# Moving the places of the matmul operands in on-chip memory: other strides for activations and weight buffers

## The chip, the cores and the metric

The kernel runs on one core of one Trainium2 chip. The metric is the device time of one execution in microseconds (us). Of the kernel before, three runs took 974.05, 974.58 and 975.09 us; the median is 974.58 us.

## The reference

One decoder layer on 256 rows of 2048 numbers, in float32. One wide projection of the input feeds three attention branches, each of which is gated, projected back, weighted by a sigmoid gate and summed; one output projection and a layer norm end it.

```python
proj = x @ w_in                                   # 256 x 2048 times 2048 x 15632
aq, ak, av, alr, agate, bq, bk, bv, bgate, cq, ck, cv, cgate, mgate = split(proj)
ya = gated_linear_attention(aq, ak, av, log_sigmoid(alr @ gla_w_up + gla_b) / 16) * silu(agate)
yb = sliding_window_attention(bq, bk, bv, swa_sinks) * silu(bgate)
yc = block_attention(cq, ck, cv) * silu(cgate)
up = einsum('bsnw,nwd->bsnd', stack([ya, yb, yc]), w_branch)      # three times 256 x 1024 x 2048
merged = sum(sigmoid(mgate + b_merge) * up)
out = merged @ w_o                                # 256 x 2048 times 2048 x 2048
x = layer_norm(2 ** 0.25 * x + out, ln_g, ln_b)
```

Nearly all of the arithmetic is in the matrix products with w_in, w_branch and w_o, whose weights (some 174 MB) are read once.

## The kernel before

**Split operands.** To come near float32 with TensorE's shorter float32r products, each operand is held as a high part and a low part (the rest), and three of the four cross products are summed: high by high, high by low, low by high.

**Chunks.** The weights are cut into chunks of 512 KB (four k-slices of 128 rows by 256 columns, or two by 512; 260 columns for the linear attention's values), in the order of their use (`seq`). `emit_chunk` loads a chunk into a `wraw` buffer over SyncE's DMA queue (line 129), casts it on ScalarE into a `whi` buffer (line 130), and subtracts on VectorE into a `wlo` buffer (line 131). There are four `wraw` buffers and three each of `whi` and `wlo`, used in turn; loads and splits run two chunks ahead of the products.

**Products with the weights standing.** In `mm3` (lines 230 to 239) 128 columns of a weight slice are loaded into TensorE as the stationary operand, and the activations of that k-slice stream past them: for the high part of the weights 512 columns (the activations' 256 high columns, then their 256 low ones, line 236), for the low part the 256 high columns (line 238). I call one such high matmul and the low one behind it a pair. A chunk of four slices and 256 columns makes 8 pairs; there are 2080 pairs in the program, 384 of them with the branch outputs `ya`, `yb`, `yc` as activations (tile `pu`), 1696 with the input `xhl`.

**Products with the activations standing.** In `nmm` (lines 274 to 282) it is the other way round: 128 columns of activations stand (`xhl`, or `mhl`, the merged result), and the weights stream past: high, low, high (lines 278, 279, 280), 260, 512 or 256 columns each. These are the values `av` (384 matmuls of 260 columns), `cv` and the first three groups of the output projection `wo` (480 of 512), and its last two groups (192 of 256).

**Places in memory.** A tile's address is its offset in bytes in each partition of the on-chip memory. What the change touches is where an operand begins; the table gives this offset modulo 512, as the two built programs have it. A buffer's k-slices of 256 columns are 1024 bytes apart and those of 512 columns 2048, so they all begin at the buffer's own place; with 260 columns they are 1040 bytes apart, and each of the four begins 16 bytes further on.

| operand | before | after |
|---|---|---|
| `xhl` and `mhl`, 16 k-slices | 416, each (2048 apart) | 224 + 96 k modulo 512: 16 places (2144 apart) |
| `ya`, `yb`, `yc`, 8 k-slices | 416, each | 224, each |
| `whi` buffers in order of use | 224, 352, 288 | 448, 128, 32 |
| `wlo` buffers in order of use | 32, 160, 96 | 160, 352, 256 |
| `wraw` buffers in order of use | 288, 480, 416, 352 | 288, 64, 480, 384 |

**Side work.** The attention branches run as jobs in small steps between the chunks (`tick`); their loads and swaps of halves go over GpSimd's DMA queue, whose descriptors stand in a scratch region of the on-chip memory (16384 bytes of each partition).

Of the kernel before, what the change touches and what calls it, by code (L numbers as in the profile page):

```python
# [9 lines left out]
F32 = mybir.dt.float32  # L10
F32R = mybir.dt.float32r
# [6 lines left out]
P = 128  # L18
S = 256
D = 2048  # L20
KT = D // P
# [6 lines left out]
RANK = 16  # L28
NV = 260
KC = 4  # L30
NWARM = 8


@with_exitstack
def kernel(ctx: ExitStack, tc: tile.TileContext, xT: bass.AP, x: bass.AP, w_in: bass.AP,
                             w_up: bass.AP, gla_b: bass.AP, norm_g: bass.AP, sinks: bass.AP, b_merge: bass.AP,
                             w_branch: bass.AP, w_o: bass.AP, ln_g: bass.AP, ln_b: bass.AP, out: bass.AP):
    nc = tc.nc

    const = ctx.enter_context(tc.tile_pool(name="const", bufs=1))  # L40
    wraw = ctx.enter_context(tc.tile_pool(name="wraw", bufs=4))
    wlo = ctx.enter_context(tc.tile_pool(name="wlo", bufs=3))
    whi = ctx.enter_context(tc.tile_pool(name="whi", bufs=3))
    acts = ctx.enter_context(tc.tile_pool(name="acts", bufs=1))
    work = ctx.enter_context(tc.tile_pool(name="work", bufs=2))
    pp = ctx.enter_context(tc.tile_pool(name="pp", bufs=2, space=PSUM))
    pa = ctx.enter_context(tc.tile_pool(name="pa", bufs=4, space=PSUM))

    # The weight chunks in the order of their use; loads and splits run ahead of the products.
    seq = []  # L50

    def deep(cols):
        return 2 if cols == 512 else KC

# [45 lines left out]
    def load_x(k0, k1):  # L100
        xs = xst[:, k0:k1, :]
        nc.sync.dma_start(xs, xT[:, k0:k1, :])
        nc.scalar.copy(xhl[:, k0:k1, 0:S], xs)
        nc.vector.tensor_tensor(xhl[:, k0:k1, S:2 * S], xs, xhl[:, k0:k1, 0:S].bitcast(F32), op=ALU.subtract)

    def emit_chunk():
        i = state["in"]
        state["in"] += 1
        src, row0, col0, cols, name = seq[i]
        kc = deep(cols)  # L110

        def shaped(t):
            return t.rearrange("p (k c) -> p k c", c=cols)
        raw = shaped(wraw.tile([P, KC * NV], F32, tag="wraw", name=f"w{name}")[:, :kc * cols])
        if name.startswith("wo4_"):
            if not last:
                last["h"] = acts.tile([P, KT, 256], F32R, tag="y", name="wlasth", bufs=2)
                last["l"] = acts.tile([P, KT, 256], F32R, tag="y", name="wlastl", bufs=2)
            k0 = KC * int(name[4:])
            hi, lo = last["h"][:, k0:k0 + KC, :], last["l"][:, k0:k0 + KC, :]  # L120
        else:
            hi = shaped(whi.tile([P, KC * NV], F32R, tag="whi", name=f"h{name}")[:, :kc * cols])
            lo = shaped(wlo.tile([P, KC * NV], F32R, tag="wlo", name=f"l{name}")[:, :kc * cols])
        view = src[row0:row0 + kc * P, col0:col0 + cols].rearrange("(k p) c -> p k c", p=P)
        cuts = [0, 1, 2] if i < 2 else [0, kc]
        for a, b in zip(cuts, cuts[1:]):
            if name.startswith("aq_"):
                load_x(row0 // P + a, row0 // P + b)
            nc.sync.dma_start(raw[:, a:b, :], view[:, a:b, :])
            nc.scalar.copy(hi[:, a:b, :], raw[:, a:b, :])  # L130
            nc.vector.tensor_tensor(lo[:, a:b, :], raw[:, a:b, :], hi[:, a:b, :].bitcast(F32), op=ALU.subtract)  # L131
        ready.append((name, hi, lo))

    def next_chunk(name):
        while state["in"] < len(seq) and state["in"] <= state["out"] + AHEAD:
            emit_chunk()
        got, hi, lo = ready[state["out"]]
        assert got == name, (got, name)
        state["out"] += 1
        return hi, lo  # L140

    # Side work, cut in steps; one step of each running job is issued between two chunks.
    jobs = []

    def tick():
# [4 lines left out]
    def wait(n):  # L150
        for _ in range(n):
            yield 1
# [2 lines left out]
        while jobs:  # L155
            tick()

    xhl = acts.tile([P, KT, 2 * S], F32R, tag="x", name="xhl")
    xst = acts.tile([P, KT, S], F32, tag="y", name="xst", bufs=2)

    # The tensor engine's clock rises only while it is busy: keep it so until the first operands are there.
    wz = const.tile([P, 512], mybir.dt.bfloat16, name="wz")
    nc.vector.memset(wz, 0.0)
    pw = pa.tile([P, 512], F32, tag="pa", name="pw")
    for _ in range(NWARM):
        nc.tensor.matmul(pw, wz[:, 0:P], wz, start=True, stop=True)
# [6 lines left out]
    nc.gpsimd.tensor_copy(ones, onesf)  # L173
    onerow = const.tile([P, 1], F32, name="onerow")
    nc.gpsimd.memset(onerow, 1.0)
    # The low-rank gate's weights three times over the rows (high, low, high parts), zeros between.
    wup3 = work.tile([96, 512], F32, tag="r", name="wup3")
    nc.gpsimd.memset(wup3, 0.0)
    for i in range(3):
# [23 lines left out]
    for i in (0, 2):  # L203
        nc.gpsimd.affine_select(mska[:, i, :], mska[:, i, :], pattern=[[-1, P]], compare_op=ALU.is_ge,
                                fill=NEG, base=0, channel_multiplier=1)
    # [row, column]: 1 where column > row; where column >= row; where column < row
    trif = work.tile([P, P], F32, tag="q1", name="trif", bufs=4)
    tril = const.tile([P, P], F32, name="tril")
    triu = const.tile([P, P], F32, name="triu")
# [98 lines left out]
    for k in range(0, KT, 2):  # L308
        hi, lo = next_chunk(f"aq_{k // 2}")
# [16 lines left out]
    def gla_job():  # L326
# [15 lines left out]
            return hl  # L342

        def sums(hl, name):
            # Sums over the partitions, the same in each row.
            pd = pa.tile([P, 512], F32, tag="pa", name=f"pd{name}")
            for e in range(2):
                nc.tensor.matmul(pd, ones, hl[:, e, :], start=e == 0, stop=e == 1)
            return pd

        def diagonal(g):
            prod = work.tile([P, 512], F32, tag="z", name=f"qk{g}")
            hs = slice(2 * g, 2 * g + 2)
            nc.vector.tensor_tensor(prod.rearrange("p (h t) -> p h t", h=2), aq[:, hs, :], ak[:, hs, :], op=ALU.mult)
            hl = halves(prod, f"d{g}")
            yield from wait(2)
            pd = sums(hl, f"d{g}")
            nc.vector.tensor_tensor(atd[:, hs, :, :], pd.rearrange("p (h t i) -> p h t i", h=2, t=2),
                                    ident[:, None, None, :].to_broadcast([P, 2, 2, P]), op=ALU.mult)
            yield 1  # L360
# [40 lines left out]
        hl = halves(e1, "1")  # L401
        yield from wait(3)
        place(0, sums(hl, "1"))

        def prep(L):
# [87 lines left out]
    def front_job():  # L493
        yield from gla_job()
        while not done:
            yield 1
        yield from keys_job()
        yield from in_turn(swa_job, 8, 6)
# [16 lines left out]
    def keys_job():  # L515
        nc.gpsimd.dma_start(ksw[0:64, :], bkv[64:128, 0, :])
        nc.gpsimd.dma_start(ksw[64:128, :], bkv[0:64, 0, :])
        yield from wait(2)
        # A key tile's values as [low parts | high parts]
        pv = pa.tile([P, 2, 2, 64], F32, tag="pa", name="pvb")  # L520
        for t in range(2):
            nc.tensor.transpose(pv[:, t, :, :], bkv[:, 1, t * P:(t + 1) * P], ident)
        nc.scalar.copy(vz[:, :, :, 64:P], pv)
        nc.vector.tensor_tensor(vz[:, :, :, 0:64], pv, vz[:, :, :, 64:P].bitcast(F32), op=ALU.subtract)
        yield from wait(2)
        for g in range(2):
            for r in range(2):
                rows = slice(64 * r, 64 * r + 64)
                src = bkv[rows, 0, :] if g == r else ksw[rows, :]
                nc.scalar.copy(ks[rows, g, 0, :], src)  # L530
                nc.vector.tensor_tensor(ks[rows, g, 1, :], src, ks[rows, g, 0, :].bitcast(F32), op=ALU.subtract)
# [1 line left out]
    yb = acts.tile([P, 8, 2 * S], F32R, tag="y", name="yb", bufs=2)  # L533

    def swa_job(hp):
        # A head's queries stand over its 64 rows as their high and low parts: products with the keys' high
        # parts twice and low parts twice give all four terms.
        g = hp // 4
        c0 = 1024 + 512 * (hp % 2)
        qs = swaw[:, c0:c0 + 512].rearrange("p (j c) -> p j c", j=2)  # L540
# [1 line left out]
        for j in range(2):  # L542
            rows = slice(64 * j, 64 * j + 64)
# [53 lines left out]
        for j in range(2):  # L597
            rows, other = slice(64 * j, 64 * j + 64), slice(64 - 64 * j, P - 64 * j)
# [127 lines left out]
    drain()  # L726
    merge(2, yc)

    mhl = acts.tile([P, KT, 2 * S], F32R, tag="x", name="mhl")
    for dg in range(8):  # L730
        ks = slice(2 * dg, 2 * dg + 2)
        nc.scalar.activation(mhl[:, ks, 0:S], merged[dg], AF.Copy, scale=0.5)
# [48 lines left out]
    parts = [next_chunk(f"wo4_{h}") for h in range(KT // KC)]  # L781
# [41 lines left out]
```

## Time and profile before

| | |
|---|---|
| median of three runs | 974.58 us |
| the profiled execution, first to last instruction | 973.3 us |
| TensorE busy with matmuls | 956.5 us (98%) |
| TensorE's weight loads | 841.5 us (86%) |
| VectorE, ScalarE, GpSimd busy | 632.6, 500.6, 93.6 us |
| mean granted TensorE clock | 0.996 |

The profile is of one execution. Its span is the time between the first and the last instruction on the chip; the measured time of a run has a little more around it (the median is 1.3 us longer than this span). Matmuls overlap in the pipeline, so the duration of one (0.39 us for 512 columns) is longer than the step from its start to the next one's start; a pace is read from starts in the timeline.

### The profile page before, as it was taken

The page shows a single profiled execution, that of the slowest core. Times are in us where ns is not written, and L with a number is a line of the kernel's source. Part 1 is how long each engine was busy: PE and PEld are TensorE (multiplying, and loading weights), DVE is VectorE, ACT ScalarE, POOL GpSimd, SP SyncE. Part 2 cuts the span into 40 slices and gives each one's busy share as a digit, 9 for nine tenths or more (in the row PEclk, how much of TensorE's full clock was granted, in tenths as well). Part 3 has the DMA queues.
Part 4 walks back from the last instruction along what each step waited for, and adds up shares of the span by engine and source line. Part 5 has one row for each costly group of instructions (what it writes and reads, how often), then busy time and mean ns, then how long its engine had stood idle before and what let it go on. Part 6 is the DMA issues. An engine that isn't in the chain of part 4 may idle for free.

```text
span 973.3 us, 14360 instructions
## 1 busy us (share of the span) xinstructions
PE 956.5 (98%) x5598; PEld 841.5 (86%) x5598; DVE 632.6 (65%) x780; ACT 500.6 (51%) x735; POOL 93.6 (10%) x127
## 2 busy tenths in 40 slices
PE   8999999999999999999999999999999999999995
PEld 5899889998888888888888888888888888888885
DVE  6544698758878888855544456665656565585556
ACT  6443574457566666644444445654445454563341
POOL 8100000003112322310000000110000000000003
PEclk9999999999999999999999999999999999999998
DMA  9766666555766666567666666487666666655652
GB/s 301 203 180 192 175 174 173 149 138 152 206 179 183 180 171 185 174 217 195 187 186 190 194 190 179 130 259 217 195 190 185 190 193 194 189 179 187 195 181 87
DMA packets 164052, 180.64 MB, mean 186 GB/s; under 512 B 6048, under 2 KB 150336, under 8 KB 163472
## 3 DMA queue, kind: packets, MB, share of 16 engines
q1 hardware_dynamic: 161552, 174.02, 61.7%
q0 software_dynamic: 2144, 5.51, 1.8%
q8 instruction: 44, 0.72, 0.3%
q10 hardware_dynamic: 288, 0.20, 0.1%
q14 instruction: 24, 0.20, 0.1%
HBM read 176.43 MB, written 2.10 MB: 183 GB/s over the span
## 4 chain that ended last, share of the span: by engine, by line
PE 95%; DVE 3%; DMA 1%; SPq 0%; POOL 0%; issue 0%; ACT 0%; DVEq 0%
PE psmg L236 18%; PE psmg L238 9%; PE pu L236 9%; PE pu L238 4%; PE psbq L236 3%; PE psag L236 3%; PE pscg L236 3%; PE pscq L236 3%; PE psck L236 3%; PE pswo L278 3%; PE pswo L280 3%; PE pswo L279 3%; PE psbg L236 2%; PE psav L278 2%; PE psav L279 2%; PE psav L280 2%
## 5 line engine op out<-in xcount | busy, mean ns | idle before, releaser
L236 PE MATMUL psmg<-xhl,hmg 128*128 128x512 f32 x768 | 269.1, 394 | 0.0
L238 PE MATMUL psmg<-xhl,lmg 128*128 128x256 f32 x768 | 214.5, 279 | 0.0
L131 DVE TENSOR_TENSOR lmg<-wmg,hmg 128x1024 fp32r<-128x1024 f32 x96 | 120.1, 1251 | 79.3 <-ACT hmg L130 79.2
L236 PEld LDWEIGHTS psmg<-xhl,hmg 128*128 128x128 f32 x768 | 144.4, 188 | 30.9
L130 ACT CAST hmg<-wmg 128x1024 fp32r<-128x1024 f32 x96 | 100.6, 1048 | 105.4 <-PE psmg L236 33.4
L238 PEld LDWEIGHTS psmg<-xhl,lmg 128*128 128x128 f32 x768 | 144.5, 188 | 0.1
L131 DVE TENSOR_TENSOR lwb<-wwb,hwb 128x1024 fp32r<-128x1024 f32 x48 | 58.8, 1224 | 40.9 <-ACT hwb L130 40.8
L130 ACT CAST hwb<-wwb 128x1024 fp32r<-128x1024 f32 x48 | 50.2, 1047 | 52.8 <-PE psmg L236 34.8
L131 DVE TENSOR_TENSOR lwo<-wwo,hwo 128x1024 fp32r<-128x1024 f32 x28 | 34.2, 1222 | 27.5 <-ACT hwo L130 27.4
L130 ACT CAST hwo<-wwo 128x1024 fp32r<-128x1024 f32 x28 | 29.4, 1050 | 41.9 <-PE pswo L280 38.5
L278 PE MATMUL pswo<-hwo,mhl 128*128 128x512 f32 (+1 forms) x128 | 47.0, 367 | 0.0
L280 PE MATMUL pswo<-hwo,mhl 128*128 128x512 f32 (+1 forms) x128 | 46.8, 366 | 0.0
L279 PE MATMUL pswo<-lwo,mhl 128*128 128x512 f32 (+1 forms) x128 | 46.8, 365 | 0.0
L236 PE MATMUL psbq<-xhl,hbq 128*128 128x512 f32 x128 | 45.6, 398 | 0.0
L236 PE MATMUL psbg<-xhl,hbg 128*128 128x512 f32 x128 | 45.2, 394 | 0.0
L236 PE MATMUL pu<-ya,hwb 128*128 128x512 f32 x128 | 45.0, 393 | 0.0
L236 PE MATMUL pu<-yb,hwb 128*128 128x512 f32 x128 | 45.0, 394 | 0.0
L236 PE MATMUL psag<-xhl,hag 128*128 128x512 f32 x128 | 44.9, 393 | 0.0
L236 PE MATMUL pu<-yc,hwb 128*128 128x512 f32 x128 | 44.6, 392 | 0.0
L236 PE MATMUL pscg<-xhl,hcg 128*128 128x512 f32 x128 | 44.4, 392 | 0.0
L236 PE MATMUL pscq<-xhl,hcq 128*128 128x512 f32 x128 | 44.4, 392 | 0.0
L236 PE MATMUL psck<-xhl,hck 128*128 128x512 f32 x128 | 44.3, 391 | 0.0
(309 smaller groups left out, 2349.5 us busy)
## 6 DMA issues: line engine op xcount, KB each, us to landing
wmg<-in_w_in_dram SPq DMA_DIRECT2D x96, 512.0 KB, 3.8
wwb<-in_w_branch_dram SPq DMA_DIRECT2D x48, 512.0 KB, 3.5
wwo<-in_w_o_dram SPq DMA_DIRECT2D x32, 512.0 KB, 4.5
wav<-in_w_in_dram SPq DMA_DIRECT2D x16, 520.0 KB, 3.7
wag<-in_w_in_dram SPq DMA_DIRECT2D x16, 512.0 KB, 3.7
wbq<-in_w_in_dram SPq DMA_DIRECT2D x16, 512.0 KB, 3.8
wbg<-in_w_in_dram SPq DMA_DIRECT2D x16, 512.0 KB, 3.7
wcq<-in_w_in_dram SPq DMA_DIRECT2D x16, 512.0 KB, 3.8
```

The lines of the kernel that those rows point to most:

```text
L130: nc.scalar.copy(hi[:, a:b, :], raw[:, a:b, :])
L131: nc.vector.tensor_tensor(lo[:, a:b, :], raw[:, a:b, :], hi[:, a:b, :].bitcast(F32), op=ALU.subtract)
L236: nc.tensor.matmul(ps, hi[:, k, c], rhs[:, k0 + k, :], start=first and k == 0, stop=False, skip_group_check=True)
L238: nc.tensor.matmul(ps[:, 0:S], lo[:, k, c], rhs[:, k0 + k, 0:S], start=False, stop=last and k == kc - 1, skip_group_check=True)
L278: nc.tensor.matmul(ps[:, t, :cols], sh, hi[:, k, :], start=kk == 0, stop=False, skip_group_check=True)
L279: nc.tensor.matmul(ps[:, t, :cols], sh, lo[:, k, :], start=False, stop=False, skip_group_check=True)
L280: nc.tensor.matmul(ps[:, t, :cols], sl, hi[:, k, :], start=False, stop=kk == KT - 1, skip_group_check=True)
```

## The change

The activations' tiles `xhl` and `mhl` get rows of 536 numbers for each k-slice, of which 512 are used; the three kinds of weight buffers get 8 numbers more (4192 bytes in place of 4160). The scratch region of GpSimd's DMA queue is halved, and with it every tile behind it begins 8192 bytes earlier, before the other shifts. The lines that are left out below are comments that the change drops.

```diff
@@ -28,6 +28,8 @@
 RANK = 16
 NV = 260
 KC = 4
+WCOLS = KC * NV + 8
+XP = 2 * S + 24
 NWARM = 8
...
-        raw = shaped(wraw.tile([P, KC * NV], F32, tag="wraw", name=f"w{name}")[:, :kc * cols])
+        raw = shaped(wraw.tile([P, WCOLS], F32, tag="wraw", name=f"w{name}")[:, :kc * cols])
...
-            hi = shaped(whi.tile([P, KC * NV], F32R, tag="whi", name=f"h{name}")[:, :kc * cols])
-            lo = shaped(wlo.tile([P, KC * NV], F32R, tag="wlo", name=f"l{name}")[:, :kc * cols])
+            hi = shaped(whi.tile([P, WCOLS], F32R, tag="whi", name=f"h{name}")[:, :kc * cols])
+            lo = shaped(wlo.tile([P, WCOLS], F32R, tag="wlo", name=f"l{name}")[:, :kc * cols])
...
-    xhl = acts.tile([P, KT, 2 * S], F32R, tag="x", name="xhl")
+    xhl = acts.tile([P, KT, XP], F32R, tag="x", name="xhl")[:, :, 0:2 * S]
...
-    mhl = acts.tile([P, KT, 2 * S], F32R, tag="x", name="mhl")
+    mhl = acts.tile([P, KT, XP], F32R, tag="x", name="mhl")[:, :, 0:2 * S]
...
-    nc = bacc.Bacc("TRN2", target_bir_lowering=False, num_devices=1)
+    nc = bacc.Bacc("TRN2", target_bir_lowering=False, num_devices=1, dynamic_dma_scratch_size=8192)
```

The instructions of every engine, their order and what they wait for are the same before and after; only addresses differ.

## Rows read from the trace of the kernel before

**Rows 1.** The page: span, busy time and share of each engine.

```profile
span 973.3 us, 14360 instructions
PE 956.5 (98%) x5598; PEld 841.5 (86%) x5598; DVE 632.6 (65%) x780; ACT 500.6 (51%) x735; POOL 93.6 (10%) x127
```

**Rows 2.** The page: the chain that ended last, by engine.

```profile
PE 95%; DVE 3%; DMA 1%; SPq 0%; POOL 0%; issue 0%; ACT 0%; DVEq 0%
```

**Rows 3.** TensorE's waits: what for, us in total, times, longest.

```profile
PE psaq L236 <- ACT haq L130: 1.6, 2, 0.9
PE pw L166 <- DVE wz L163: 1.3, 1, 1.3
PE psbg L238 <- DVE lbg L131: 1.2, 1, 1.2
```

**Rows 4.** Matmul groups by shape: count, busy us, mean ns, idle before.

```profile
L236 PE MATMUL psmg<-xhl,hmg 128*128 128x512 f32 x768 | 269.1, 394 | 0.0
L238 PE MATMUL psmg<-xhl,lmg 128*128 128x256 f32 x768 | 214.5, 279 | 0.0
```

**Rows 5.** Timeline, TensorE: first pair of four chunks that follow each other.

```profile
267.37 0.39 PE L236 MATMUL psmg<-xhl,hmg 128*128 128x512 f32 x1
...
270.18 0.39 PE L236 MATMUL psmg<-xhl,hmg 128*128 128x512 f32 x1
...
272.91 0.39 PE L236 MATMUL psmg<-xhl,hmg 128*128 128x512 f32 x1
...
275.68 0.40 PE L236 MATMUL psmg<-xhl,hmg 128*128 128x512 f32 x1
```

**Rows 6.** Windows of these chunks: us, engines' busy us, granted clock, DMA share, GB/s.

```profile
267.37:270.18 2.81, 2.81 (x18) 2.46 (x17) 2.74 (x6) 2.69 (x9) 1.02 (x2) 1.00 0.78 215
270.18:272.91 2.73, 2.73 (x19) 2.42 (x17) 2.43 (x6) 1.95 (x6) 0.00 (x0) 1.00 0.81 206
272.91:275.68 2.77, 2.77 (x19) 2.44 (x17) 1.86 (x2) 1.05 (x1) 0.00 (x0) 1.00 0.34 71
```

**Rows 7.** Timeline, TensorE: first matmuls of two chunks of `av`, 24 apart.

```profile
77.28 0.28 PE L278 MATMUL psav<-hav,xhl 128*128 128x260 f32 x1
...
80.17 0.29 PE L278 MATMUL psav<-hav,xhl 128*128 128x260 f32 x1
```

**Rows 8.** Timeline, TensorE: 12 matmuls of `wo` with 512 columns.

```profile
893.94 0.40 PE L278 MATMUL pswo<-hwo,mhl 128*128 128x512 f32 x1
...
896.73 0.39 PE L278 MATMUL pswo<-hwo,mhl 128*128 128x512 f32 x1
```

**Rows 9.** Timeline, TensorE: `wo` with 256 columns: 24 matmuls, later 15.

```profile
947.03 0.28 PE L278 MATMUL pswo<-hwo,mhl 128*128 128x256 f32 x1
...
949.87 0.28 PE L278 MATMUL pswo<-wlasth,mhl 128*128 128x256 f32 x1
...
958.49 0.28 PE L278 MATMUL pswo<-wlasth,mhl 128*128 128x256 f32 x1
...
960.29 0.28 PE L278 MATMUL pswo<-wlasth,mhl 128*128 128x256 f32 x1
```

**Rows 10.** Groups of the splits: busy us, mean ns, idle before and its releaser.

```profile
L131 DVE TENSOR_TENSOR lmg<-wmg,hmg 128x1024 fp32r<-128x1024 f32 x96 | 120.1, 1251 | 79.3 <-ACT hmg L130 79.2
L130 ACT CAST hmg<-wmg 128x1024 fp32r<-128x1024 f32 x96 | 100.6, 1048 | 105.4 <-PE psmg L236 33.4
```

**Rows 11.** DMA issues: count, KB each, median us to landing; GpSimd's queue, the loads of x.

```profile
wmg<-in_w_in_dram SPq DMA_DIRECT2D x96, 512.0 KB, 3.8
swaw<-ql POOLq DMA_DIRECT2D x16, 64.0 KB, 2.0
q0 software_dynamic: 2144, 5.51, 1.8%
L742 POOL DMA_DIRECT2D hx<-in_x_dram x2: 582/597/612, 420.9 to 640.3; - x2
```

## The prediction

> **What bounds the kernel now.** I read the page's busy shares first, then the chain of waits, then TensorE's own waits, and then the pace of the matmuls in the timeline. TensorE is busy for 956.5 of 973.3 us [rows 1] and makes 95% of the chain that ended last [rows 2]. Its three longest waits for another engine sum to 4.1 us, 2.9 of them at the start [rows 3]. So the time is, but for the few per cent that the chain gives to others, the sum of the steps from one matmul's start to the next. The groups by shape show the two that dominate, 768 of 512 columns and 768 of 256 in the gates' products alone, with no idle time before them [rows 4], but their durations overlap and cannot be added; only starts can.
>
> The starts show what this change can touch. Four chunks of the gates' products follow each other, each of 8 pairs, and differ in nothing but the weight buffers they use [rows 5]. The first begins at 267.37 us and the second at 270.18: 2.81 us for 8 pairs, 351 ns each (buffers at 224 and 32). The second takes 2.73 us, 341 ns (352 and 160). The third takes 2.77 us, 346 ns (288 and 96). The same work at the same granted clock, 1.00 in all three windows [rows 6], has three paces 3% apart. Contention with the other engines does not order them: the fastest chunk ran beside the busiest DMA (share 0.81), the middle one beside the idlest (0.34) and the least work of VectorE and ScalarE (1.86 and 1.05 us) [rows 6]. What goes with the pace is the place of the weights against that of the activations, which begin at 416 in every k-slice. I take from this that the stream of activations and the load of the next weights disturb each other, by an amount that hangs on their places and on how far one is ahead of the other. Within a chunk all 8 pairs have the same places, and the pace settles.
>
> The Trainium skill says otherwise: in "SBUF — State Buffer", section "Who interferes with whom", TensorE has two independent read ports, one for the stream and one for the weight load, and never waits on another reader; and "TensorE: Matmul & The Clock Gate", section "Wait — 56ns, not 53.3ns?", gives N ÷ 2.4 GHz plus about 2.5 ns from start to start. By that a pair would be 215.8 + 109.2 = 325 ns at any place, and the change would be worth nothing. The trace does not agree: 341 to 351 ns, by buffer. What the rule leaves alive is the first rival below.
>
> **The change part by part.** No instruction moves, so the sum has one large term, TensorE's pace, and some that I put at nothing.
>
> *Pairs with xhl: 1696.* Now three settled paces, mean (2.81 + 2.73 + 2.77) / 24 = 346.3 ns [rows 5]. After the change the activations of slice k begin at 224 + 96 k, so no two pairs of neighbouring slices have the same relation, and no pace settles over a chunk. The trace has no pair of this kind, so I bound it. Below: all pairs as the fastest buffer now, 341 ns, which is 1696 × −5.3 = −9.0 us. Above: all as the slowest, 351 ns, 1696 × 4.7 = +8.0 us. The nearest rows between these are the matmuls with the activations standing. Those of `av` stream from weights whose slices begin 16 bytes apart, so they see four places in each chunk: 2.89 us for 24, 120.4 ns for 260 columns [rows 7]. Beside them, `wo` with 512 columns takes 2.79 / 12 = 232.5 ns [rows 8] and with 256 columns 2.84 / 24 = 118.3 ns [rows 9], one place to a chunk. A column thus costs (232.5 − 118.3) / 256 = 0.446 ns, and `av` cut to 256 columns would be 120.4 − 4 × 0.446 = 118.6 ns. So many places are neither better nor worse than one of the three, 118.6 against 118.3. They are a little better than the last group of `wo`, where both operands begin at 416 and the step settles at 1.80 / 15 = 120.0 ns [rows 9].
>
> Put together, a 512-column and a 256-column step of this kind make 232.5 + 118.6 = 351.1 ns, 4.8 ns above the pairs' mean now. This says that the settled pairs are somewhat luckier than the usual step, and that unsettled ones would drift towards the usual. But `wo` loads its weights from one tile all the time, and its 512-column steps have no low part between them, so I believe it by half: 348.7 ns, +2.4 ns, 1696 × 2.4 = +4.1 us.
>
> *Pairs with the branch outputs: 384.* `ya`, `yb` and `yc` keep one place, 224, and the buffers move against it, so these settle again, at other relations. Between 341 and 351 ns that is −2.0 to +1.8 us; I take 0, the mean of three unknown paces.
>
> *The 1056 matmuls with activations standing.* They change places too. The steps of [rows 7 to 9], cut to 256 columns, lie within 118.3 to 120.0 ns, so 576 short ones could move by some ±1 ns and 480 long ones by ±2: ±1.5 us, taken as 0.
>
> *Splits and loads.* The casts and subtractions write to other places, and the loads land at others. A subtraction takes 1.25 us and a cast 1.05 [rows 10] of a chunk's 2.77 us; a load lands in 3.8 us [rows 11] and is issued two chunks ahead. The cover is TensorE's chunk. If it went, say by a cast and a subtraction of twice the length, VectorE with its other work would become late; TensorE waited for a split once after the start, for 1.2 us [rows 3]. I put it at 0, with 0 to +2 us.
>
> *The halved scratch of GpSimd's queue.* It moves 2144 packets and 1.8% of the engines' time; its loads of x are issued at 420.9 and 640.3 us, hundreds of us before the residual needs them; the swaps of query halves land in 2.0 us [rows 11] and stand four steps ahead of their use, some 11 us. Even if each of the 16 swaps took twice as long, nothing would wait: 0.
>
> *Sum.* +4.1 us on the profiled execution's 973.3 us span, 977.4 us. The median of the runs is 1.3 us above that span, so I predict 974.6 + 4.1 = 978.7 us.
>
> **The rivals.**
>
> *No change: the mean over places is what it was.* The three settled paces would be a fair sample, each pair would just draw from the same range, and the slow ones pay for the fast. For it: `av`'s many places cost what `wo`'s three do, 118.6 against 118.3 ns. Against it: 232.5 + 118.6 is above the pairs' mean. By the skill's two pages above there would be no change either, for another reason. Time: 974.6, ±2 us. Chance 0.25.
>
> *Faster: the settled pace is a resonance, and many places break it.* The mechanism is that in a settled chunk the load of the next weights meets the stream in each pair at the same point, again and again; where the relation changes with k, a bad meeting is not repeated. For it: two of three buffers are slower than the third by 5 and 10 ns a pair, and the pace falls by steps of 5 ns as the buffers' places rise by 64 bytes, so that places further on may be better still; the last group of `wo` gets its 120.0 ns with everything at one place. Against it: `av` shows no such gain against 118.3 ns. It decides once more than half of the relations behave as the fastest does; if two thirds do, 1696 × 2/3 × −5.3 = −6.0 us, 968.6 us; if all do, with the branch outputs' pairs, −11.0 us, 963.6 us. Chance 0.33.
>
> *Slower in full.* The pairs with xhl go all the way to 351.1 ns, as the steps of `wo` and `av` have it: 1696 × 4.8 = +8.1 us, 982.7 us. It is the far end of my forecast. If a bad branch-output pace and the splits came on top, 1.8 + 1 us, it would be 985.5 us.
>
> **How the numbers follow.** Slower than before, by the forecast's mechanism in half or in full: 0.42. No change: 0.25. Faster: 0.33. The forecast's own range is 976.6 to 983. As both signs hold much of the chance, the range for 8 times in 10 goes over all cases: from 965.0, which leaves out the last tenth, near every pair at the fastest pace, to 984.5. A measurement of this kernel can tell 0.2% from no change, 1.95 us, so "within" is 972.6 to 976.5 us. The rival without change lies wholly in it, the two others almost wholly outside, so the chances are those of the cases.
>
> **What would show it.** In the profile after, TensorE should still be 98% busy and its waits the same few us; the pairs with xhl should no longer have three paces by buffer but steps that change from k-slice to k-slice, with a mean near 349 ns over a few chunks; those with the branch outputs should again settle, at three paces. A mean near 346 says no change, one below 345 the resonance. I am wrong in the mechanism if pairs with xhl still run evenly within a chunk, since then the places were not what made the three paces; or if TensorE's waits on the splits have grown, since then the cost lies on VectorE and ScalarE.

## The result, and the profile after

The changed kernel takes 982.12 us (four runs, 982.04 to 982.63) against 974.84 us for the kernel before: a ratio of 1.0076, 95% interval 1.0061 to 1.0090. It is slower by 7.3 us. I predicted 978.7 us, slower, with a range of 965.0 to 984.5.

The head of the page after answers to [rows 1]; the columns are the same.

```profile
span 980.4 us, 14360 instructions
PE 964.8 (98%) x5598; PEld 844.3 (86%) x5598; DVE 632.8 (65%) x780; ACT 500.4 (51%) x735; POOL 92.9 (9%) x127
```

TensorE's busy time has grown by 8.3 us, the other engines' by nothing that matters (VectorE 632.6 to 632.8 us, ScalarE 500.6 to 500.4). Its longest waits for other engines are the same three as in [rows 3], 3.5 us in all where they were 4.1:

```profile
PE psaq L238 <- ACT haq L132: 1.3, 1, 1.3
PE pw L168 <- DVE wz L165: 1.3, 1, 1.3
PE psbg L240 <- DVE lbg L133: 0.9, 1, 0.9
```

The two large groups answer to [rows 4] (after the change the lines of `mm3` are two further down); the last number before the idle time is the mean duration in ns:

```profile
L238 PE MATMUL psmg<-xhl,hmg 128*128 128x512 f32 x768 | 272.5, 397 | 0.0
L240 PE MATMUL psmg<-xhl,lmg 128*128 128x256 f32 x768 | 215.7, 281 | 0.0
```

The durations went from 394 to 397 and from 279 to 281 ns. The starts tell the pace. These are the first pairs of the four chunks of [rows 5] (268.39, 271.19, 273.99, 276.79), and between them three neighbouring pairs of the second chunk:

```profile
268.39 0.39 PE L238 MATMUL psmg<-xhl,hmg 128*128 128x512 f32 x1
...
271.19 0.39 PE L238 MATMUL psmg<-xhl,hmg 128*128 128x512 f32 x1
...
272.24 0.40 PE L238 MATMUL psmg<-xhl,hmg 128*128 128x512 f32 x1
...
272.60 0.39 PE L238 MATMUL psmg<-xhl,hmg 128*128 128x512 f32 x1
...
272.94 0.40 PE L238 MATMUL psmg<-xhl,hmg 128*128 128x512 f32 x1
...
273.99 0.40 PE L238 MATMUL psmg<-xhl,hmg 128*128 128x512 f32 x1
...
276.79 0.40 PE L238 MATMUL psmg<-xhl,hmg 128*128 128x512 f32 x1
```

Where [rows 5] had 2.81, 2.73 and 2.77 us for 8 pairs, all three steps are now 2.80 us, 350 ns a pair; and within the second chunk, pairs that follow each other take 0.36 and 0.34 us. The three paces are gone, the fast one with them. The steps are not random, though. The chunk at 268.39 takes 343, 350, 348, 354, 357, 353, 346 and 346 ns for its 8 pairs, and the chunk at 286.41, six chunks on, has the same buffers, and its activations' places are 8 × 96 = 768 bytes further on, a multiple of 256: it takes the same eight times to the nanosecond. Over all pairs in the trace that nothing interrupts, those with `xhl` have a mean of 346.5 ns before (1656 pairs) and 351.1 after (1655); those with the branch outputs 347.0 and 348.8. Added over the whole trace, the pairs with `xhl` have grown by 6.6 us (5.7 in the steps behind a high matmul, 0.9 in those behind a low one) and those with the branch outputs by 0.7 us; the matmuls with the activations standing have lost 0.3 us. The sum with the rest is 7.05 us, which is the two spans' 7.1 us.

### The profile page after: what moved, and what is told of

It reads as the page before. It is cut to its first block, busy times and chain, and to the rows that moved or that the text cites. A ratio compares the mean times of both kernels' runs of the same rounds, so it can differ in the third digit from the quotient of the medians.

```text
span 980.4 us, 14360 instructions
## 1 busy us (share of the span) xinstructions
PE 964.8 (98%) x5598; PEld 844.3 (86%) x5598; DVE 632.8 (65%) x780; ACT 500.4 (51%) x735; POOL 92.9 (9%) x127
## 4 chain that ended last, share of the span: by engine, by line
PE 94%; DVE 4%; issue 1%; ACT 0%; DMA 0%; POOL 0%; SPq 0%; DVEq 0%
PE psmg L238 18%; PE psmg L240 9%; PE pu L238 9%; PE pu L240 4%; PE psbq L238 3%; PE psag L238 3%; PE pscg L238 3%; PE psck L238 3%; PE pscq L238 3%; PE pswo L282 3%; PE pswo L280 3%; PE pswo L281 3%; PE psaq L238 2%; PE psav L281 2%; PE psav L280 2%; PE psav L282 2%
## 5 line engine op out<-in xcount | busy, mean ns | idle before, releaser
L238 PE MATMUL psmg<-xhl,hmg 128*128 128x512 f32 x768 | 272.5, 397 | 0.0
```

The costliest lines, as they stand in the source:

```text
L238: nc.tensor.matmul(ps, hi[:, k, c], rhs[:, k0 + k, :], start=first and k == 0, stop=False, skip_group_check=True)
```

## The experiments

Two theories stood at first. Mine: a pair's pace hangs on the relation of the two operands' places, and where that changes with every k-slice the pace does not settle. The rival: some places are dear in themselves, such as those with remainder 0 modulo 64, which no operand of the products had before (all had 32) and half of them have now. All kernels below halve GpSimd's scratch as the change does. Pair paces are means over some 1600 uninterrupted pairs with `xhl`.

**The parts alone.** Three kernels take one part of the change each: the activations' slices, the weight buffers, the scratch.

```diff
+XP = 2 * S + 24                     # e1: xhl and mhl, as in the change; buffers as before
+WCOLS = KC * NV + 8                 # e2: wraw, whi, wlo, as in the change; slices as before
+..., dynamic_dma_scratch_size=8192) # e3: this alone (also in e1, e2)
```

> Only the activations' slices move (2144 bytes apart); weight buffers and branch outputs stand where they stood, modulo 512. Theory (a pair's pace hangs on the relation of the two operands' places, and only where the relation stays from slice to slice does the pace settle): the pairs with xhl no longer settle, 351 in place of 346.5 ns, 1696 of them: +7.7 us, about 982.3 us; the branch outputs' pairs stay at 347. Rival (places with a remainder of 0 modulo 64 are dear, and before all operands had a remainder of 32): half of the slices now have 0, and none of the buffers, so about half of the change's 7.3 us: 978.5 us, with the slices of remainder 0 the slow ones.

> Only the weight buffers move (4192 bytes each); the activations' slices are 2048 bytes apart as before, all at one place. Theory: the pace settles again, by buffer, at the relations that the branch outputs' pairs have in the changed kernel (there 347 to 351 ns, mean about 348.9): 2080 pairs times 2.3 ns, +4.9 us, 979.7 us, with three paces by buffer. Rival (many places as such do no harm, the remainder of 0 modulo 64 does): four of the six buffers have 0 now, so about half of the change's loss or more, 978 to 982 us, and the buffers at remainder 32 run at the old pace.

> Only the scratch of GpSimd's queue is halved: everything behind it begins 8192 bytes earlier, at the same places modulo 512. Theory: no change, 974.8 us within 0.2%, and the same three paces of 341, 346 and 351 ns. Rival (the halved scratch or the absolute address costs): up to the change's 7 us, 977 to 982 us.

| kernel | us | ratio, 95% interval | pair with xhl, ns |
|---|---|---|---|
| slices alone | 980.58 | 1.0063 (1.0048 to 1.0078) | 349.7 |
| buffers alone | 978.00 | 1.0033 (1.0020 to 1.0045) | 348.4: 350.0, 347.0, 348.8 by buffer |
| scratch alone | 974.91 | 1.0001 (0.9992 to 1.0010) | 346.5: 350.7, 342.4, 346.6 by buffer |

The halved scratch and the shift of all addresses by 8192 bytes cost nothing that can be seen. The slices alone cost 5.7 us, halfway between my 7.7 and the rival's half of the change, 3.65. By place, the pairs of slices with remainder 0 take 350.2 ns and those with remainder 32 take 349.2; in the kernel before the same slices have 345.8 and 347.3. So both kinds have lost, which the rival does not say, but this run alone does not settle it. The buffers alone cost 3.1 us although nothing moves from slice to slice: they stand at relations that are just less good. So a part of the loss needs no moving slices at all. (Three of the six weight buffers have remainder 0 here, not four, one in each pair of a high and a low buffer, so this run cannot test the rival.) Nor does one relation always give even steps: the chunk at 273.03 us has 340 and 353 or 354 ns by turns from its second pair on. The parts do not add: 5.7 + 3.1 is more than 7.3.

**A map of relations.** Each buffer gets 5120 bytes, and a chunk's number says where in it the chunk begins.

```diff
+def places(i):
+    return 16 * (i % 8), 16 * (i // 8 % 8)      # numbers of 4 bytes: high part, low part
...
+            oh, ol = places(i)
+            hi = shaped(whi.tile([P, 1280], ...)[:, oh:oh + kc * cols])
+            lo = shaped(wlo.tile([P, 1280], ...)[:, ol:ol + kc * cols])
```

> A map: activations at one place (32) in all slices, each chunk's high part 64 times i bytes after that, its low part 64 times i/8 bytes (i the chunk's number, both modulo 8), so that all 64 relations in steps of 64 bytes occur, each in some chunks of 8 pairs. Theory: each relation has a pace of its own, from 341 or less to 356 ns, and a chunk's pace is the same where the relation comes again; the relations of the kernel before have 351 (320 and 128 bytes after the activations), 346 (384 and 192) and 341 (448 and 256) here too; the mean over all is near 349 to 351. Rival (absolute places count, not relations): those three do not come out in this order, as all places here differ from before.

The mean over all 1978 uninterrupted pairs is 349.6 ns (one run, 980.27 us). Relations 256 bytes apart came out alike: the four cells that are (192, 0) modulo 256 have 341.2, 341.9, 341.6 and 341.8 ns. Put together modulo 256, the high part's distance from the activations down, the low part's across, mean ns of a pair (113 to 138 pairs each):

| | 0 | 64 | 128 | 192 |
|---|---|---|---|---|
| 0 | 350.2 | 347.0 | 349.3 | 350.5 |
| 64 | 350.6 | 351.9 | 351.5 | 350.4 |
| 128 | 351.5 | 347.2 | 350.7 | 353.4 |
| 192 | 341.6 | 347.3 | 349.1 | 352.6 |

The timeline shows the ends. First a chunk at (448, 0): its first pair, its eighth, and the first of the next chunk; then the same of a chunk at (128, 192):

```profile
425.20 0.39 PE L244 MATMUL pscq<-xhl,hcq 128*128 128x512 f32 x1
...
427.60 0.39 PE L244 MATMUL pscq<-xhl,hcq 128*128 128x512 f32 x1
...
427.94 0.40 PE L244 MATMUL pscq<-xhl,hcq 128*128 128x512 f32 x1
...
478.25 0.40 PE L244 MATMUL psck<-xhl,hck 128*128 128x512 f32 x1
...
480.72 0.40 PE L244 MATMUL psck<-xhl,hck 128*128 128x512 f32 x1
...
481.07 0.40 PE L244 MATMUL psck<-xhl,hck 128*128 128x512 f32 x1
```

8 pairs in 2.74 us (427.94 − 425.20) against 2.82 (481.07 − 478.25). The kernel before stood at (192, 0), (64, 128) and (128, 192) modulo 256. Two of its three paces came out again, 341.6 and 351.5 ns; the third did not, 353.4 here against 346.6. The second map below has the three relations of the buffers alone at 350.9, 348.1 and 348.4 ns, where that kernel has 350.0, 347.0 and 348.8. But the map shows why a spread costs: one cell in sixteen is near 341, and the kernel before had a third of its chunks there. The mean of its three paces was no fair sample of relations.

A relation also has to last. In the map's chunks at (192, 0) the first pair takes 346.6 ns, the second 344.4 and from the fourth on 340 (means of some 18 chunks). In the kernel with the slices alone 215 pairs with `xhl` have this relation, each between pairs of other relations: their mean is 350.0 ns, and only 19 take 343 ns or less. One of them, with the pair behind it:

```profile
279.90 0.40 PE L237 MATMUL psmg<-xhl,hmg 128*128 128x512 f32 x1
...
280.26 0.39 PE L237 MATMUL psmg<-xhl,hmg 128*128 128x512 f32 x1
```

It takes 0.36 us where a settled pair takes 0.34.

**Whether the relation can be chosen.** All chunks at the best cell, all at the worst, and the best cell with both operands moving by 96 bytes from slice to slice, so that the operands begin at 16 places modulo 512 but keep their relation.

```diff
+def places(i):
+    return 48, 0                    # e7; e9: 32, 48; e8: as e7 and
+            # e8, chunks multiplied with xhl in pairs, xhl and mhl as in the change:
+                k0, pitch = row0 // P, cols + 24
+                o += 24 * k0 % 128
+                return t[:, o:o + kc * pitch].rearrange("p (k c) -> p k c", c=pitch)[:, :, 0:cols]
```

> All chunks stand at the fastest relation of the map (high part 192 bytes after the activations, low part 0, modulo 512), the slices of the activations at one place. Theory (the relation sets the pace, and it settles): 341.3 ns for all 2080 pairs against 346.5 now, -10.8 us, 964.0 us, with no difference between the three buffers. Rival (the fast chunks of the map were fast by what came before them, or because their buffer is): three paces remain, 346 to 350 on average, 974 to 980 us.

> As the kernel with the fastest relation, but the activations' slices are 2144 bytes apart as in the change, and the slices of the weights move with them by 96 bytes each, so that operands begin at 16 places modulo 512 while their relation stays the same; the weights of the branch outputs stand still, as those do. Theory (only the relation counts): as fast as without the moving, 964 us within 2 us. Rival (many places are dear as such, or those of remainder 0 modulo 64 are): the pairs with xhl at 350 to 351 ns, 979 to 981 us.

> All chunks stand at the slowest relation of the map (high part 128 bytes after the activations, low part 192), the slices at one place. Theory: settled, but at 353.8 ns, 2080 times 7.3 ns, +15 us, 990 us: slower than the changed kernel although nothing moves from slice to slice. Rival (a settled pace is lucky, a moving one dear): at most the mean of the map, 349.6 ns, 981 us.

> A second map in steps of 32 bytes over 256 bytes for both parts, as the first map shows the same pace at relations 256 bytes apart. Theory: again a few relations near 341 ns, 192 and 0 among them, the rest at 346 to 354; the mean at 349 to 351, about 980 us. If a relation below 340 ns exists at an odd multiple of 32 it is seen here. Rival (remainders modulo 64 count as such): the relations with odd multiples of 32 are all slower, or all faster, than those with even ones.

| kernel | us | ratio, 95% interval | pair with xhl, ns |
|---|---|---|---|
| e7, all at (192, 0) | 965.85 | 0.9912 (0.9893 to 0.9930) | 341.8 |
| e8, (192, 0), moving together | 977.29 | 1.0027 (1.0017 to 1.0036) | 349.9 |
| e9, all at (128, 192) | 976.59 | 1.0021 (1.0012 to 1.0031) | 347.6 |
| e6, map in steps of 32 | 980.00 (one run) | | 349.6 |

The best relation is real: the steps are even through chunks that follow each other, 2.72 us each, and the kernel is faster than those before and after the change.

```profile
265.75 0.39 PE L244 MATMUL psmg<-xhl,hmg 128*128 128x512 f32 x1
...
268.47 0.39 PE L244 MATMUL psmg<-xhl,hmg 128*128 128x512 f32 x1
...
271.19 0.39 PE L244 MATMUL psmg<-xhl,hmg 128*128 128x512 f32 x1
...
273.91 0.39 PE L244 MATMUL psmg<-xhl,hmg 128*128 128x512 f32 x1
```

The second map found no better one: (192, 0) again leads with 342.8 ns; odd multiples of 32 lie among the others, from 345.2 to 353.7, which speaks against the rival of remainders. With remainder 0 for both parts of the weights the mean is 349.0 ns, with 32 for both 350.1, with one of each 349.6 and 350.0; and the first map, where every operand has 32, has the same mean, 349.6, as this one.

The worst relation missed by 13 us, and the timeline of e9 says why. One relation can settle at two paces:

```profile
331.30 0.40 PE L244 MATMUL pu<-ya,hwb 128*128 128x512 f32 x1
...
334.12 0.40 PE L244 MATMUL pu<-ya,hwb 128*128 128x512 f32 x1
...
344.01 0.39 PE L244 MATMUL psmg<-xhl,hmg 128*128 128x512 f32 x1
...
346.78 0.39 PE L244 MATMUL psmg<-xhl,hmg 128*128 128x512 f32 x1
```

Eight pairs take 2.82 us (353 ns) up to a place where side work of a branch stands between two chunks, and 2.77 us (346 ns) behind it, with nothing moved. The same holds at (192, 0): 1645 of 1978 pairs of e7 take 340 ns, and 232 take 350. So the pace hangs on the relation and on what ran before it. That agrees with the third buffer of the kernel before at 346 and the map's cell at 353, which have this relation; no run shows what entry leads to which.

Moving together missed too: 349.9 ns, no better than the slices alone (349.7), and close to the 350 to 351 that the rival of many places said of these pairs. But in it a high part is loaded while the slice before it still streams, and so stands 288 bytes after that stream, not 192. The trace of e8 shows this load (PEld) begin with the low matmul before its own:

```profile
268.11 0.19 PEld L252 LDWEIGHTS psmg<-xhl,hmg 128*128 128x128 f32 x1
...
268.11 0.28 PE L254 MATMUL psmg<-xhl,lmg 128*128 128x256 f32 x1
```

The next kernel takes that away.

**Which relation counts, and its period.** In e10 the high parts begin 96 bytes earlier, so that each load stands as in e7 against the stream that it runs beside. In e11 and e5 only the activations' stride of the kernel before is changed, to 2304 and to 2560 bytes: places 256 bytes apart by turns, and one place.

```diff
+                oh = 24             # e10, in e8's pairs with xhl
+XP = 2 * S + 64                     # e11; e5: 2 * S + 128
```

> As the kernel in which the weights' slices move with the activations', but the high parts begin 96 bytes earlier (96 bytes after their own slice's activations), so that a high part, which is loaded while the slice before it still streams, stands 192 bytes after the stream beside which it is loaded, as in the fastest kernel; the low parts are loaded beside their own slice's stream and stay at 0. Theory (a load disturbs the stream that it runs beside, and only the relation of those two counts): the pairs with xhl settle again except at the two turns in a chunk where the slice number jumps, about 343 ns, 1608 times 7 ns less than in the kernel before it: 966 to 970 us. Rival (a stream's own places, or the step from one stream's place to the next, count too): no better than 349 ns, 976 to 978 us.

> The kernel before, with the activations' slices 2304 bytes apart, so that they begin at two places modulo 512, 256 bytes apart. Theory (the period is 256 bytes, as the first map has it): every relation stays, the three paces of 341, 346 and 351 ns too, 974.7 us within 0.3%. Rival (the period is 512 bytes): the relation changes with every slice, the pairs with xhl run at 350 ns, 980 to 982 us.

> The kernel before, with the activations' slices 2560 bytes apart: another stride, all slices at one place modulo 512. Theory: no change, 974.7 us within 0.2%, the three paces stay. Rival (the stride of 2048 itself is what is fast, or a longer period counts): 978 to 982 us, like the changed kernel's slices alone.

| kernel | us | ratio, 95% interval | pair with xhl, ns |
|---|---|---|---|
| e10, lagged | 978.39 | 1.0037 (1.0024 to 1.0050) | 348.7 |
| e11, slices 2304 bytes apart | 975.00 | 1.0003 (0.9993 to 1.0013) | 346.5 |
| e5, slices 2560 bytes apart | 974.62 | 0.9999 (0.9990 to 1.0009) | 346.5 |

The period is 256 bytes, not the 512 in which the change is described: in e11 the activations begin at two places modulo 512, and the three paces of [rows 5] stay, 2.82, 2.72 and 2.77 us:

```profile
267.41 0.39 PE L237 MATMUL psmg<-xhl,hmg 128*128 128x512 f32 x1
...
270.23 0.39 PE L237 MATMUL psmg<-xhl,hmg 128*128 128x512 f32 x1
...
272.95 0.39 PE L237 MATMUL psmg<-xhl,hmg 128*128 128x512 f32 x1
...
275.72 0.40 PE L237 MATMUL psmg<-xhl,hmg 128*128 128x512 f32 x1
```

My theory for e10 fell: 978.39 us where it said 966 to 970, and 348.7 ns a pair, near the rival's 349. The relation of a load to the stream beside it is not all that counts. The timeline has the fifth, sixth and seventh pair of two chunks that follow each other:

```profile
416.98 0.39 PE L253 MATMUL pscq<-xhl,hcq 128*128 128x512 f32 x1
...
417.33 0.39 PE L253 MATMUL pscq<-xhl,hcq 128*128 128x512 f32 x1
...
417.67 0.39 PE L253 MATMUL pscq<-xhl,hcq 128*128 128x512 f32 x1
...
419.77 0.39 PE L253 MATMUL pscq<-xhl,hcq 128*128 128x512 f32 x1
...
420.12 0.39 PE L253 MATMUL pscq<-xhl,hcq 128*128 128x512 f32 x1
...
420.46 0.39 PE L253 MATMUL pscq<-xhl,hcq 128*128 128x512 f32 x1
```

The second chunk repeats the first 2.79 us later, step for step, though it begins 384 bytes further on modulo 512. (The chunks behind it do the same.) So places modulo 256 or 512 do not count in themselves; as 384 is a multiple of 128, the repeat says nothing of remainders modulo 64. And the sequence does settle, with steps of 344 to 353 ns in each chunk; but where streams step by 96 bytes its mean is 349 ns. Either the step from one stream to the next counts, or a load's relation to its own stream as well; I have not told these apart.

**The best version.** The matmuls with the activations standing take 234.4 ns for 512 columns in e7, and the first map shows them faster elsewhere. This kernel is e7 with those chunks moved.

```diff
+    if name.startswith(("cv", "wo")):
+        return (112, 112) if name.startswith("wo3") else (64, 64)
```

> The fastest relation for the pairs, and for the matmuls with the activations standing the places that the first map shows fastest: both parts of the streaming weights 256 bytes after the activations where they have 512 columns (228.8 ns in 4 chunks of the map, 234.4 in the fastest kernel), 448 where they have 256 (114.4 in one chunk, 117.8). Theory: 480 times 5.6 and 96 times 3.4 ns less, -3.0 us, 962.9 us. Rival (those few chunks were fast by what came before them): no change against 965.9 us.

It takes 961.97 us, a ratio of 0.9878 (0.9863 to 0.9892) to the kernel before. Against [rows 8], 12 matmuls of 512 columns take 2.72 us, 226.7 ns:

```profile
880.62 0.39 PE L288 MATMUL pswo<-hwo,mhl 128*128 128x512 f32 x1
...
883.34 0.39 PE L288 MATMUL pswo<-hwo,mhl 128*128 128x512 f32 x1
```

480 × (234.4 − 226.8) = 3.6 us of the 3.9 us to e7. The group of 256 columns whose chunks were moved did not gain (117.8 ns): the one chunk of the map was no measure. (The last group stands in tiles of its own and was not moved.)

## Why the prediction was right, and what it had wrong

- *The bound.* That the time is the sum of TensorE's steps held: 7.05 of the 7.1 us lie in them, and the waits on other engines are as before.
- *Pairs with xhl, the one large term.* Direction and place held; the size was too small, +2.4 ns predicted and +4.6 measured (346.5 to 351.1), 1696 × 4.6 = 7.8 us for my 4.1. (All 1696 together, the interrupted ones too, grew by 6.6 us.) The step that failed is that I believed the sum of the other matmuls' steps "by half": 351.1 ns, 232.5 + 118.6, is what came. So the case that I called slower in full, 982.7 us, came nearest. But that this sum meets the pace looks like luck: the other kernels with slices 96 bytes apart have 349.7, 349.9 and 348.7 ns (e1, e8, e10). And "by half" was a guess between two numbers.
- *Its reason.* I said that unsettled pairs drift to the usual step. The runs show two things here. The fastest relation needs some pairs to settle, and where the relation changes with each slice it is worth nothing (350.0 ns in the slices alone, 340 settled). And fixed relations cost too, if they are others: the buffers alone lose 3.1 us, as the three paces of before were better than the map's mean, 349.6 ns, because one of them is the best cell of sixteen. So the sign was in part luck, the three relations that the kernel happened to have. Of the 4.6 ns, 3.1 are the distance to the map's mean, and 1.5 lie above it; how much each of the two things has in them is not shown.
- *No change.* Its premise, that three paces are a fair sample, is what the map refutes; that each pair draws from the range by its own relation is refuted by the 215 pairs of the slices alone. The rule of the Trainium skill ("SBUF — State Buffer", section "Who interferes with whom") by which TensorE waits on no other reader, so that places would not matter, does not agree with e7 and e12, which change places alone and gain 0.9 and 1.2%; here the measurement decides.
- *Faster: many places break a resonance.* Wrong: the best pace is a settled one (e7), and every kernel with slices 96 bytes apart is slower than before.
- *Branch outputs.* Taken as 0; 384 × 1.8 = +0.7 us. They stand at one relation to a buffer, but only some chunks settle to even steps, as I expected of all: the one at 629.72 us runs at 346 to 347 ns, the one at 738.78 at 340 and 353 by turns.
- *Activations standing, splits, loads, scratch.* Taken as 0; −0.3 us for the first, none to be seen for the others, and the scratch alone is within 0.1%.

## What to carry to other kernels

Where TensorE loads new weights for every matmul, look at starts in the timeline by buffer before touching anything: paces that differ by buffer and not by work were here a matter of places. Then choose a relation rather than spread, and keep it from pair to pair: here one relation of weights to activations in sixteen (modulo 256 bytes) is worth 0.9% of the whole, and 1.2% with the other products' places chosen too, by buffers of one size, a multiple of 512 bytes, and a fixed start in each. Map the relations in one run by letting the chunk's number set the place, and then run the candidate alone, since a few chunks in a map can mislead (e9, and the 256-column group of e12).

## What the runs showed of the hardware that I had not expected

- Where the two parts of the weights stand against the activations moves a pair's mean pace between 340 and 354 ns, with a period of 256 bytes, at the same granted clock, and not in the order of the other engines' work [rows 6].
- One relation has more than one settled pace: 353 and 346 ns at (128, 192) in e9, 340 and 350 at (192, 0) in e7. In e10 the branch outputs stand at (192, 0) and have 341.3 ns in the first branch and 349.9 in the two others. What chooses among them is open.
- A settled sequence repeats to the nanosecond or two, chunk after chunk, at other absolute places (e10); its steps need not be even (340 and 353 ns by turns in the buffers alone).
